# Attention on one core: 16 of 32 head pairs have their Q and K transposed by DMA inside SBUF, and VectorE computes up to eight groups of exponentials

## The chip, the cores and the metric

The kernel runs on one core of a Trainium2 chip. A core has five engines, each with its own stream of instructions: TensorE (PE in the profile; PEld is its weight load), VectorE (DVE), ScalarE (ACT), GpSimd (POOL) and SyncE (SP). SP computes nothing here; it issues the DMA transfers, which 16 DMA engines carry out. [...] each of them, SP included, works through its own program in order. The metric is the device time of one execution in microseconds (us).

## The reference

Plain attention, 8 batches of 8 heads, 512 positions of dimension 64, in and out in float32:

```python
batch, heads, seq, dim = 8, 8, 512, 64
scale = 1.0 / np.sqrt(q.shape[-1])
scores = np.einsum('bhqd,bhkd->bhqk', q, k) * scale
scores = scores - scores.max(axis=-1, keepdims=True)
attn = np.exp(scores)
attn = attn / attn.sum(axis=-1, keepdims=True)
return np.einsum('bhqk,bhkd->bhqd', attn, v)
```

The 64 heads are worked on as 32 pairs (g = 0 to 31). A pair has 8 blocks of scores of 128 keys x 512 queries, and two blocks make a group of 128 x 1024. The kernel skips the maximum: the scores of these inputs are small enough for exp in float32. The row sum comes from a column of ones beside V.

## The kernel before

Each pair goes through these stages: SP loads q, k, v in float32; POOL casts them to fp16 (`qkp`, `vp`); PE transposes q and k, 8 blocks of 128 x 128 into one PSUM bank (`tp`), and DVE copies them to SBUF (`tqk`); PE multiplies the scores (`st`, three PSUM buffers of two banks); ACT takes the exponential into fp16 (`pt`); PE multiplies with V (`o`), seven units of 128 rows to a bank; DVE divides by the row sums into `ring`, and SP stores it.

```python
def feed(g):                      # once a pair, at the first scores of pair g
    load(g + 5, "kqv")
    cast_qk(g + 3)
    cast_v(g + 2)

def transposes(g, n, bank):
    if n == 0:
        tqk[g] = tpool.tile([P, 2, S], FP16, tag="tqk", name=f"tqk_{g}")
        tps[g] = ps_x.tile([P, 2, NI, P], FP16, tag=f"x{bank}", name=f"tp_{g}")
    n = 1 - n
    for i in range(NI):
        nc.tensor.transpose(tps[g][:, n, i, :], qkp[g][:, n, i, :], ident)      # L348

def copy(g):
    ...
    nc.vector.tensor_copy(                                                      # L355
        out=tqk[g][:, :, :], in_=tps.pop(g).rearrange("p n i c -> p n (i c)"))

def scores(m, on_dve):
    ...
        nc.tensor.matmul(st[:, x, :], kc, qc, start=True, stop=True)            # L374
        ...
    if on_dve:
        raised[m] = {"st": st, "pt": pt}
        return
    nc.scalar.activation(                                                       # L379
        out=pt[:, 0:size, :], in_=st[:, 0:size, :], func=EXP, scale=scale)
```

Some groups don't go to ACT: DVE computes their exponential itself. One instruction (`raise_`, L393) reads the scores from PSUM and turns them into an integer whose upper bits are the exponent; six passes (`pass_`: L406 and L417 for the bits, four times L428 for a polynomial of fourth degree) work on it in SBUF. That is seven instructions to a group, and they stand between the copies and the normalisations (L440, L441) of the same engine.

The order of PE's and DVE's instructions is made when the kernel is built. `Plan` steps through a model of the two engines and of ACT, with durations in ns, and writes down what each engine does next; the kernel then issues its instructions in that order.

```python
class Plan:
    SLOT, EXP, EXP_DONE, EXP_FIXED = 216, 853, 1085, 51
    ...
    COPY, NORM, NORM_COLUMN = 700, 380, 67
    RAISE, PASSES, LATE = 1216, (867, 822, 1400, 1400, 1400, 1372), 700
    HURRY = 1200

    def for_dve(self, m):             # does group m go to DVE?
        g = self.groups[m][0][0]
        return (m > 5 and g < self.pairs - 3 and not self.passes
                and not any(x[1] == "raise" for x in self.ready))

    def step_dve(self, t):
        now = [x for x in self.ready if x[0] <= t]
        if now:
            ...                       # a copy, a normalisation or a raise
        elif self.passes:             # else the next pass, if no such work comes soon
            m, s = self.passes[0]
            if min((x[0] for x in self.ready), default=1e9) > t + self.PASSES[s] - self.LATE:
                ...
```

Buffers: six float32 tiles each for q, k and v (`load`), three `qkp`, four `tqk`, thirty `pt` for ACT and three (`pd`) for DVE's groups.

Of the kernel before, what the change touches and what calls it, by code (L numbers as in the profile page):

```python
# [9 lines left out]
FP16 = mybir.dt.float16  # L10
U32 = mybir.dt.uint32

EXP = mybir.ActivationFunctionType.Exp
# [3 lines left out]
class Plan:  # L17
# [10 lines left out]

    SLOT, EXP, EXP_DONE, EXP_FIXED = 216, 853, 1085, 51
    INTO, OUT_OF = 95, 105
    TRANSPOSE, V_UNIT = 225, 130
    TO_ACT, TO_DVE, TO_PE = 275, 210, 60
    COPY, NORM, NORM_COLUMN = 700, 380, 67
    RAISE, PASSES, LATE = 1216, (867, 822, 1400, 1400, 1400, 1372), 700
    HURRY = 1200
    STEP = 5
    FIRST_UNIT = 4

    def __init__(self, groups, pairs, first):
        self.groups, self.pairs = groups, pairs
        self.pe, self.act, self.dve = 6000, 4800 + first * 904, 5800
        self.m, self.tiled = first, True
        self.read = []
        self.exps = {}
        for m in range(first):
            self.exps[m] = 4800 + m * 904 + self.EXP_DONE
            self.read.append(self.exps[m])
        self.tq = {0: 5800}  # L50
        self.next_t = 1
        self.part_t = 0
        self.banks = [5100, 5800]
        self.todo = [(g, h) for g in range(pairs) for h in range(2)]
        self.head = None
        self.units = self.FIRST_UNIT
        self.member = {b: m for m, grp in enumerate(groups) for b in grp}
        self.ready = []
        self.passes = []
        self.steps = []  # L60

    def note(self, t, *what):
# [15 lines left out]
    def for_dve(self, m):  # L78
        g = self.groups[m][0][0]
        return (  # L80
            m > 5
            and g < self.pairs - 3
            and not self.passes
            and not any(x[1] == "raise" for x in self.ready)
        )

    def scores(self, t):
        m, grp = self.m, self.groups[self.m]
        slots = 2 if len(grp) == 2 and 0 < grp[0][0] and grp[0][2] == grp[1][2] else 1
        on_dve = self.for_dve(m)  # L90
        if m % 4 == 0 and grp[0][0] > 0 and len(grp) == 2:
            self.note(t, "feed", grp[0][0])
        self.note(t, "scores", m, on_dve)
        t += (0 if self.tiled else self.INTO) + self.SLOT * slots
        self.tiled = True
        if on_dve:
            self.ready.append((t + self.TO_DVE, "raise", (m,)))
            self.read.append(1e9)
        else:
            begin = max(self.act, t + self.TO_ACT)  # L100
            self.act = begin + self.EXP * len(grp) // 2 + self.EXP_FIXED
            self.exps[m] = self.act + self.EXP_DONE - self.EXP - self.EXP_FIXED
            self.read.append(self.exps[m])
        self.m += 1
        self.pe = t
# [61 lines left out]
    def step_pe(self, t):  # L167
        if self.m == len(self.groups):
            self.values(t)
            return  # L170
        g = self.groups[self.m][0][0]
        backlog = self.act - t
        one, two = self.free() <= t, self.free(1) <= t
        if one and (two or backlog < self.HURRY):
            return self.scores(t)
        if not one and backlog < 1300 and self.free() < t + 150:
            return
        if self.part_t:
            return self.transposes(t)
        if (  # L180
            self.next_t < self.pairs
            and self.next_t <= g + 1
            and t >= self.ready_kq(self.next_t)
            and self.bank(t) is not None
        ):
            return self.transposes(t)
        if not self.values(t) and one:
            self.scores(t)
# [4 lines that stand above are left out]
            job = min(now, key=lambda x: (x[1] != "raise", x[0]))  # L193
            self.ready.remove(job)
            _, kind, what = job
            self.note(t, kind, *what)
            if kind == "norm":
                self.dve = t + self.NORM + self.NORM_COLUMN * what[1]
                self.banks[what[2]] = self.dve + self.TO_PE
            elif kind == "copy":  # L200
                self.dve = t + self.COPY
                self.banks[what[1]] = self.tq[what[0]] = self.dve + self.TO_PE
            else:
                self.dve = t + self.RAISE
                self.read[what[0]] = self.dve + self.TO_PE
                self.passes += [(what[0], s) for s in range(len(self.PASSES))]
        elif self.passes:
            m, s = self.passes[0]
            if min((x[0] for x in self.ready), default=1e9) > t + self.PASSES[s] - self.LATE:
                self.passes.pop(0)  # L210
                self.note(t, "pass", m, s)
                self.dve = t + self.PASSES[s]
                if s == len(self.PASSES) - 1:
                    self.exps[m] = self.dve + self.TO_PE

    def run(self):
        t = 0
# [12 lines left out]
def kernel(  # L230
# [7 lines left out]
    nc = tc.nc  # L238
    B, H, S, D = q.shape
    P = 128  # L240
# [21 lines left out]
    cpool = ctx.enter_context(tc.tile_pool(name="const", bufs=1))  # L262
    lpool = ctx.enter_context(tc.tile_pool(name="load", bufs=6))
    qpool = ctx.enter_context(tc.tile_pool(name="qk16", bufs=3))
    tpool = ctx.enter_context(tc.tile_pool(name="tqk", bufs=4))
    ppool = ctx.enter_context(tc.tile_pool(name="pt", bufs=30))
    dpool = ctx.enter_context(tc.tile_pool(name="pd", bufs=3))
    wpool = ctx.enter_context(tc.tile_pool(name="work", bufs=1))
# [14 lines left out]
    qkp = {}  # L283
    tqk = {}
# [5 lines left out]
    first = {}  # L290
    last = {}

    def source(src, g):
        b, h = g // ppb, 2 * (g % ppb)
        return src[b, h : h + 2].rearrange("h (p i) d -> p h i d", i=NI)

    def load_tile(g, name):
        t = lpool.tile(
            [P, 2, NI, D],
            FP32,  # L300
            tag=f"{name}32",
            name=f"{name}32_{g}",
            bufs=6,
        )
        raw.setdefault(g, {})[name] = t
        return t

    def load(g, names):
        if g >= NP:
            return  # L310
        for name in names:
            src = {"q": q, "k": k, "v": v}[name]
            t = load_tile(g, name)
            if name == "v" and g in HALVED:
                for h in range(2):
                    nc.sync.dma_start(out=t[:, h], in_=source(src, g)[:, h])
                continue
            nc.sync.dma_start(out=t[:, :, :, :], in_=source(src, g))

    def cast_v(g):  # L320
        if g >= NP:
            return
        nc.gpsimd.tensor_copy(out=vps[g % NV][:, :, :, 0:D], in_=raw[g]["v"][:, :, :, :])  # L323

    def cast_qk(g):
        if g >= NP:
            return
        t = qpool.tile([P, 2, NI, P], FP16, tag="qkp", name=f"qkp_{g}")
        for n, name in ((1, "k"), (0, "q")):
            eng = nc.vector if (g, name) == (1, "q") else nc.gpsimd  # L330
            eng.tensor_copy(  # L331
                out=t[:, n].rearrange("p i (h d) -> p h i d", h=2),
                in_=raw[g][name][:, :, :, :],
            )
        qkp[g] = t

    def feed(g):
        load(g + 5, "kqv")
        cast_qk(g + 3)
        cast_v(g + 2)  # L340
# [260 lines left out]
    with tc.manual_schedule():  # L601
        first_loads()
        load(1, "kq")
        load(0, "v")
        for g in range(2, 5):
            load(g, "kq")
            load(g - 1, "v")
        load(4, "v")
        make_identity(nc, ident)
        for n in range(NV):  # L610
            nc.vector.memset(vps[n][:, :, :, D : D + 1], 1.0)
        first_pair()
        cast_qk(1)
        cast_v(0)
        cast_qk(2)
        cast_v(1)
        feed(0)
        do = {
            "transposes": transposes,
            "scores": scores,  # L620
            "values": values,
            "feed": feed,
            "raise": raise_,
            "copy": lambda g, b: copy(g),
            "pass": pass_,
            "norm": lambda u, n, b: normalise(u, n),
        }
        for what, *args in Plan(groups, NP, 3).run():
            do[what](*args)
# [30 lines left out]
```

The softmax here doesn't subtract the row's maximum and nothing guards it: scores larger than these inputs give would overflow.

## Time and profile before

| | |
|---|---|
| device time, median of 3 runs | 123.18 us (123.15 to 123.48) |
| span of the profiled execution | 121.7 us |
| ACT busy | 114.4 us (94%) |
| PE busy, PEld busy | 108.1 us, 67.6 us |
| DVE busy | 98.5 us (81%) |
| POOL busy | 73.9 us (61%) |
| moved by DMA | 33.82 MB, mean 278 GB/s |
| exponentials in ACT's main loop, on DVE | 120 instructions, 6 groups |

A row of groups in the profile reads: line, engine, operation, tile written <- tiles read, partitions x elements, x count | busy us, mean ns of one | idle us of that engine just before them, and what ended most of it. PE's matmuls and ACT's activations overlap their neighbours, so that the mean of one is longer than the step from one to the next. A line of digits divides the span into 40 equal slices and gives the busy share of each in tenths. Releasers, which name what ended a wait, are inferred from semaphores.

### The profile page before, as it was taken

What the parts mean: (1) busy time and instruction counts of PE and PEld (TensorE: products, weight loads), DVE (VectorE), ACT (ScalarE), POOL (GpSimd) and SP (SyncE); (2) the same over time, 40 slices, a digit from 0 to 9 for tenths busy, and PEclk for the clock granted to TensorE, in tenths of its full rate; (3) what the DMA queues carried; (4) which work ended last, traced back from release to release, by engine and by line L of the source; (5) the groups of instructions that cost most, each with busy time, mean ns of one, the idle gap of its engine ahead of it and who ended that gap; (6) DMA issues with size and microseconds to landing.
All of it is one profiled execution on the core that took longest, in us unless ns stands there. A gap on an engine that the chain in (4) does not pass through costs nothing.

```text
span 121.7 us, 3951 instructions
## 1 busy us (share of the span) xinstructions
PE 108.1 (89%) x1557; PEld 67.6 (56%) x1557; DVE 98.5 (81%) x171; ACT 114.4 (94%) x127; POOL 73.9 (61%) x101
## 2 busy tenths in 40 slices
PE   7979788889899798998998998889999998999970
PEld 2556455547466465664565564556655655556550
DVE  1456899989989898699999998986979899876451
ACT  4599999999999999999999999999999999999970
POOL 2368969998487977396587577366794377300000
PEclk9999999999999999999999999999999999999995
DMA  3899999999999989998899967899979995113234
GB/s 117 273 363 384 385 376 384 387 275 282 370 374 352 311 284 318 335 347 276 238 312 297 318 226 251 268 348 343 325 239 281 348 330 196 64 52 126 93 110 152
DMA packets 35603, 33.82 MB, mean 278 GB/s; under 512 B 2688, under 2 KB 35584, under 8 KB 35584
## 3 DMA queue, kind: packets, MB, share of 16 engines
q1 hardware_dynamic: 35152, 33.24, 83.1%
q10 hardware_dynamic: 432, 0.33, 0.9%
q8 instruction: 12, 0.20, 0.7%
q14 instruction: 7, 0.06, 0.2%
HBM read 25.17 MB, written 8.39 MB: 276 GB/s over the span
## 4 chain that ended last, share of the span: by engine, by line
ACT 54%; PE 22%; issue 19%; DVE 2%; ACTq 0%
ACT pt L379 54%; PE st L374 8%; PE o L462 6%; PE st_0a L510 3%; PE tp L348 2%; PE st L553 1%; DVE tqk L353 1%; PE o_last L477 1%; DVE ring L441 1%; PE tp_qb L548 0%; DVE qt L590 0%; DVE obl L490 0%; PE tp_qa L548 0%; PE st_0a L553 0%; DVE rc L440 0%
## 5 line engine op out<-in xcount | busy, mean ns | idle before, releaser
L379 ACT ACTIVATE pt<-st 128x1024 f16<-128x1024 f32 (+1 forms) x120 | 109.4, 1327 | 0.1
L374 PE MATMUL st<-tqk 64*128 64x512 f16 x248 | 48.1, 384 | 7.4 <-ACT pt L379 6.5
L462 PE MATMUL o<-vp,pt 128*128 128x65 f16 x1008 | 46.9, 195 | 1.7 <-ACT pt L379 1.3
L462 PEld LDWEIGHTS <-pt 128*128 128x128 f16 x1008 | 37.0, 98 | 18.8 <-issue 15.0
L331 POOL CAST qkp<-k 128x512 f16<-128x512 f32 x31 | 25.3, 815 | 24.2 <-DMA k<-in_k_dram 18.1
L323 POOL CAST vp<-v 128x512 f16<-128x512 f32 x32 | 27.4, 859 | 1.0 <-DMA v<-in_v_dram 0.9
L374 PEld LDWEIGHTS <-tqk 64*128 64x128 f16 x248 | 13.3, 93 | 20.7 <-issue 12.7
L331 POOL CAST qkp<-q 128x512 f16<-128x512 f32 x30 | 22.7, 756 | 2.4 <-DMA q<-in_q_dram 2.3
L441 DVE TENSOR_TENSOR ring<-o,rc 128x448 f32<-128x448 f32 (+2 forms) x37 | 22.6, 611 | 1.3
L355 DVE COPY tqk<-tp 128x1024 f16<-128x1024 f16 x30 | 20.5, 685 | 3.1 <-PE tp L348 2.8
L348 PE MATMUL tp<-ident,qkp 128*128 128x128 f16 x248 | 19.5, 220 | 0.0
L348 PEld LDWEIGHTS <-qkp 128*128 128x128 f16 x248 | 14.0, 98 | 6.9 <-issue 4.7
L428 DVE SCALAR_TENSOR_TENSOR y<-y,m 128x1024 f32<-128x1024 f32 x12 | 15.9, 1321 | 0.0
L440 DVE RECIPROCAL rc<-o 128x7 f32<-128x7 f32 (+2 forms) x37 | 7.3, 198 | 9.3 <-PE o L462 9.1
L393 DVE TENSOR_SCALAR z<-st 128x1024 uint32<-128x1024 f32 x6 | 7.3, 1221 | 1.1 <-PE st L374 1.1
L428 DVE SCALAR_TENSOR_TENSOR y<-m 128x1024 f32<-128x1024 f32 x6 | 8.2, 1361 | 0.0
L428 DVE SCALAR_TENSOR_TENSOR pt<-y,e 128x1024 f16<-128x1024 f32 x6 | 7.7, 1279 | 0.0
L417 DVE TENSOR_SCALAR e<-z 128x1024 uint32<-128x1024 uint32 x6 | 6.1, 1024 | 0.0
L406 DVE TENSOR_SCALAR m<-z 128x1024 uint32<-128x1024 uint32 x6 | 4.6, 765 | 0.0
L510 PE MATMUL st_0a<-const-bfloat16-1.0 128*128 128x512 bf16 (+1 forms) x11 | 3.5, 482 | 0.8 <-PEq L644 0.8
L510 PEld LDWEIGHTS <-const-bfloat16-1.0 128*128 128x128 bf16 x15 | 1.9, 143 | 2.4 <-issue 2.4
L526 ACT ACT_TABLE_LOAD x1 | 1.3, 1283 | 1.7 <-PEq L644 1.7
(43 smaller groups left out, 18.6 us busy)
## 6 DMA issues: line engine op xcount, KB each, us to landing
out_dram<-ring SPq DMA_DIRECT2D x63, 128.0 KB, 3.8
k<-in_k_dram SPq DMA_DIRECT2D x31, 256.0 KB, 4.8
q<-in_q_dram SPq DMA_DIRECT2D x31, 256.0 KB, 4.9
v<-in_v_dram SPq DMA_DIRECT2D x27, 256.0 KB, 5.3
v<-in_v_dram SPq DMA_DIRECT2D x10, 128.0 KB, 4.4
k<-in_k_dram ACTq DMA_DIRECT2D x2, 128.0 KB, 2.9
q<-in_q_dram SPq DMA_DIRECT2D x2, 128.0 KB, 2.6
out_dram<-obl SPq DMA_DIRECT2D x1, 64.0 KB, 1.8
```

Source lines behind the costliest of these rows:

```text
L323: nc.gpsimd.tensor_copy(out=vps[g % NV][:, :, :, 0:D], in_=raw[g]["v"][:, :, :, :])
L331: eng.tensor_copy(out=t[:, n].rearrange("p i (h d) -> p h i d", h=2), in_=raw[g][name][:, :, :, :],)
L348: nc.tensor.transpose(tps[g][:, n, i, :], qkp[g][:, n, i, :], ident)
L355: nc.vector.tensor_copy(out=tqk[g][:, :, :], in_=tps.pop(g).rearrange("p n i c -> p n (i c)"))
L374: nc.tensor.matmul(st[:, x, :], kc, qc, start=True, stop=True)
L379: nc.scalar.activation(out=pt[:, 0:size, :], in_=st[:, 0:size, :], func=EXP, scale=scale)
L393: nc.vector.tensor_scalar(out=r["z"][:, :, :], in0=r["st"][:, :, :], scalar1=scale * 1.4426950408889634 * 2.0**23, scalar2=(127 + SHIFT) * ...
L428: nc.vector.scalar_tensor_tensor(out=r["pt"][:, :, :] if n == 3 else r["y"][:, :, :], in0=mant if n == 0 else r["y"][:, :, :], scalar=QUAR ...
L440: nc.vector.reciprocal(out=rc[:, 0:n], in_=o[:, x : x + n, D : D + 1])
L441: nc.vector.tensor_tensor(out=ring[:, u % NU : u % NU + n, :], in0=o[:, x : x + n, 0:D], in1=rc[:, 0:n].broadcast_to([P, n, D]), op=AluOp. ...
L462: nc.tensor.matmul(os[u // 7][:, u % 7, :], blocks[(g, c, h)][:, y * P : (y + 1) * P], vps[g % NV][:, h, c, :], start=(c == 0), stop=(c == ...
L510: nc.tensor.matmul(dst[:, 0:n], ones[:, 0:P], ones[:, 0:n], start=True, stop=True)
```

## The change

Of the pairs 5 to 28, those whose number isn't a multiple of three (16 pairs in all, with pair 5 the first) get their transposed q and k by a DMA transpose from `qkp` to `tqk`, inside SBUF. SP issues it at the feed two pairs ahead, before the loads of that feed. PE's transposes and DVE's copy of these pairs fall away, and `tqk` gets a fifth buffer. On DVE, at most eight groups of exponentials are placed (there was no number before; the old order came to six). And the model from which the order is made has new durations: most have two numbers now, one for when the engine can go on and one for when the result is there. The transfers are for taking work from PE and DVE; the room on DVE is for taking exponentials from ACT.

The diff, with cuts marked:

```diff
-    SLOT, EXP, EXP_DONE, EXP_FIXED = 216, 853, 1085, 51
+    SLOT, EXP, EXP_DONE, EXP_FIXED = 216, 853, 181, 64
     ...
-    COPY, NORM, NORM_COLUMN = 700, 380, 67
-    RAISE, PASSES, LATE = 1216, (867, 822, 1400, 1400, 1400, 1372), 700
-    HURRY = 1200
+    COPY, NORM, RAISE = (615, 700), (307, 390), (1145, 1225)
+    NORM_COLUMN, PASS_DONE = 67, 80
+    PASSES = (690, 950, 1335, 1335, 1335, 1250)
+    FIRST_EXP = 5260
     ...
+    BY_DMA = (5, 7, 8, 10, 11, 13, 14, 16, 17, 19, 20, 22, 23, 25, 26, 28)
+    LATE_NORM, LATE_COPY, HURRY, SOON, BACKLOG = 200, 500, 1400, 220, 1000
+    LAST_PAIRS, AHEAD, MARGIN, SLACK, MOST = 3, 0, 1, 2000, 8
     ...
-        self.tq = {0: 5800}
+        self.tq = {0: 5800, **{g: 0 for g in self.BY_DMA}}
     ...  (for_dve)
-            and g < self.pairs - 3
-            and not self.passes
+            and g < self.pairs - self.LAST_PAIRS
+            and len(self.passes) <= self.AHEAD
+            and len(self.on_dve) < self.MOST
     ...  (step_pe)
+        while self.part_t == 0 and self.next_t in self.BY_DMA:
+            self.next_t += 1
     ...
-        if not one and backlog < 1300 and self.free() < t + 150:
+        if not one and backlog < self.BACKLOG and self.free() < t + self.SOON:
     ...  (step_dve)
-            if min((x[0] for x in self.ready), default=1e9) > t + self.PASSES[s] - self.LATE:
+            end = t + int(self.MARGIN * self.PASSES[s])
+            late = {"copy": self.LATE_COPY, "norm": self.LATE_NORM, "raise": self.LATE_NORM}
+            if all(x[0] > end - late[x[1]] for x in self.ready):
     ...
-                    self.exps[m] = self.dve + self.TO_PE
+                    self.exps[m] = end + self.PASS_DONE + self.TO_PE + self.SLACK
     ...
-    tpool = ctx.enter_context(tc.tile_pool(name="tqk", bufs=4))
+    tpool = ctx.enter_context(tc.tile_pool(name="tqk", bufs=5))
     ...
+    def transpose_by_dma(g):
+        if g not in Plan.BY_DMA:
+            return
+        tqk[g] = tpool.tile([P, 2, S], FP16, tag="tqk", name=f"tqk_{g}")
+        nc.sync.dma_start_transpose(
+            out=tqk[g].rearrange("p n (i c) -> p (n i) c", c=P),
+            in_=qkp[g].rearrange("p n i c -> p (n i c)"),
+        )
+
     def feed(g):
+        transpose_by_dma(g + 2)
         load(g + 5, "kqv")
         cast_qk(g + 3)
         cast_v(g + 2)
```

More of the change, by code (lines that the diff above doesn't have):

```diff
@@ L34 @@
     TO_ACT, TO_DVE, TO_PE = 275, 210, 60
-    COPY, NORM, NORM_COLUMN = 700, 380, 67
-    RAISE, PASSES, LATE = 1216, (867, 822, 1400, 1400, 1400, 1372), 700
-    HURRY = 1200
+    COPY, NORM, RAISE = (615, 700), (307, 390), (1145, 1225)
+    NORM_COLUMN, PASS_DONE = 67, 80
+    PASSES = (690, 950, 1335, 1335, 1335, 1250)
+    FIRST_EXP = 5260
     STEP = 5
     FIRST_UNIT = 4
+    BY_DMA = (5, 7, 8, 10, 11, 13, 14, 16, 17, 19, 20, 22, 23, 25, 26, 28)
+    LATE_NORM, LATE_COPY, HURRY, SOON, BACKLOG = 200, 500, 1400, 220, 1000
+    LAST_PAIRS, AHEAD, MARGIN, SLACK, MOST = 3, 0, 1, 2000, 8
     def __init__(self, groups, pairs, first):
         self.groups, self.pairs = groups, pairs
-        self.pe, self.act, self.dve = 6000, 4800 + first * 904, 5800
+        self.pe, self.act, self.dve = 7000, self.FIRST_EXP, 7000
         self.m, self.tiled = first, True
@@ L47, in __init__ @@
         for m in range(first):
-            self.exps[m] = 4800 + m * 904 + self.EXP_DONE
+            self.act += self.EXP + self.EXP_FIXED
+            self.exps[m] = self.act + self.EXP_DONE
             self.read.append(self.exps[m])
-        self.tq = {0: 5800}
+        self.tq = {0: 5800, **{g: 0 for g in self.BY_DMA}}
         self.next_t = 1
@@ L59, in __init__ @@
         self.passes = []
+        self.on_dve = []
         self.steps = []
@@ L96, in scores @@
         if on_dve:
+            self.on_dve.append(m)
             self.ready.append((t + self.TO_DVE, "raise", (m,)))
@@ L101, in scores @@
             self.act = begin + self.EXP * len(grp) // 2 + self.EXP_FIXED
-            self.exps[m] = self.act + self.EXP_DONE - self.EXP - self.EXP_FIXED
+            self.exps[m] = self.act + self.EXP_DONE
             self.read.append(self.exps[m])
@@ L197, in step_dve @@
             if kind == "norm":
-                self.dve = t + self.NORM + self.NORM_COLUMN * what[1]
-                self.banks[what[2]] = self.dve + self.TO_PE
+                more = self.NORM_COLUMN * what[1]
+                self.dve = t + self.NORM[0] + more
+                self.banks[what[2]] = t + self.NORM[1] + more + self.TO_PE
             elif kind == "copy":
-                self.dve = t + self.COPY
-                self.banks[what[1]] = self.tq[what[0]] = self.dve + self.TO_PE
-            else:
-                self.dve = t + self.RAISE
-                self.read[what[0]] = self.dve + self.TO_PE
+                self.dve = t + self.COPY[0]
+                self.banks[what[1]] = self.tq[what[0]] = t + self.COPY[1] + self.TO_PE
+            else:
+                self.dve = t + self.RAISE[0]
+                self.read[what[0]] = t + self.RAISE[1] + self.TO_PE
                 self.passes += [(what[0], s) for s in range(len(self.PASSES))]
@@ L208, in step_dve @@
             m, s = self.passes[0]
-            if min((x[0] for x in self.ready), default=1e9) > t + self.PASSES[s] - self.LATE:
+            end = t + int(self.MARGIN * self.PASSES[s])
+            late = {"copy": self.LATE_COPY, "norm": self.LATE_NORM, "raise": self.LATE_NORM}
+            if all(x[0] > end - late[x[1]] for x in self.ready):
                 self.passes.pop(0)
                 self.note(t, "pass", m, s)
-                self.dve = t + self.PASSES[s]
+                self.dve = end
                 if s == len(self.PASSES) - 1:
-                    self.exps[m] = self.dve + self.TO_PE
+                    self.exps[m] = end + self.PASS_DONE + self.TO_PE + self.SLACK
     def run(self):
```

## The prediction

> **What bounds the kernel now.** I read the page first: busy shares, then the chain that ended last, then the groups; after that the timeline of ScalarE (ACT), the waits of the SyncE queue (SP) and a table by window. The lines that carry it, from the page:
>
> ```profile
> PE 108.1 (89%) x1557; PEld 67.6 (56%) x1557; DVE 98.5 (81%) x171; ACT 114.4 (94%) x127; POOL 73.9 (61%) x101
> DMA  3899999999999989998899967899979995113234
> ...
> ACT 54%; PE 22%; issue 19%; DVE 2%; ACTq 0%
> ...
> L379 ACT ACTIVATE pt<-st 128x1024 f16<-128x1024 f32 (+1 forms) x120 | 109.4, 1327 | 0.1
> ...
> L355 DVE COPY tqk<-tp 128x1024 f16<-128x1024 f16 x30 | 20.5, 685 | 3.1 <-PE tp L348 2.8
> L348 PE MATMUL tp<-ident,qkp 128*128 128x128 f16 x248 | 19.5, 220 | 0.0
> ```
>
> ACT's main group has 109.4 us of busy time and 0.1 us of idle time before its instructions. Its timeline, from the answer on that engine, shows the group as one unbroken piece (start, length), and the whole end of the kernel behind it:
>
> ```profile
> 8.41 109.42 ACT L379 ACTIVATE pt<-st 128x1024 f16<-128x1024 f32 x120
> 119.08 0.37 ACTq L497 DMA_DIRECT2D out_dram<-obl  x1
> ```
>
> So from 8.41 to 117.83 us the exponential is the bound, without a hole. The mean of 1327 ns is not what one costs, because neighbours overlap. 118 of the 120 are full and 2 are half tiles, worth 119 full ones, and 109.42 / 119 = 0.92 us is the step. Everything before 8.41 and the 3.9 us after 117.83 are head and tail, which the change leaves alone.
>
> The windows of the stretch in which pairs are loaded and cast, and of the tail (length, busy of PE, PEld, DVE, ACT, POOL, clock, DMA share, GB/s), show the second resource that is near its limit:
>
> ```profile
> 10.00:98.00 88.00, 80.53 (x1193) 50.81 (x1190) 79.44 (x120) 88.00 (x97) 64.70 (x83) 1.00 0.97 318
> 98.00:121.70 23.70, 19.08 (x307) 12.24 (x304) 15.54 (x29) 19.83 (x23) 4.98 (x7) 0.95 0.42 136
> ```
>
> ACT is busy 88.00 of 88.00 us, and the DMA engines 0.97 at 318 GB/s. They can move more than that: the early slices of the page show 384 to 387 GB/s. The third tight place is SP, which issues every load and store in program order. Its waits in the same stretch, the longest lines:
>
> ```profile
> SPq L449 <- DVE ring L441: 5.9, 8, 1.4
> SPq L318 <- POOL qkp L331: 3.4, 6, 1.1
> SPq L318 <- DMA v<-in_v_dram: 2.9, 9, 0.6
> SPq L449 <- DMA q<-in_q_dram: 2.0, 6, 0.5
> SPq L318 <- DMA q<-in_q_dram: 2.0, 5, 0.8
> ```
>
> With the smaller ones of that answer (1.2, 1.2, 0.7, four times 0.4, 0.2) that makes 21.1 us of waiting in 88 us. The rest is issuing, 0.37 to 0.5 us for each plain transfer in SP's timeline.
>
> [...]
>
> **The change part by part.**
>
> Removed from PE: 16 pairs of 8 transposes. 19.5 / 31 = 0.63 us a pair, 16 x 0.63 = 10.1 us of PE. Worth nothing by itself: PE already feeds ACT with 0.1 us of idle time.
>
> Removed from DVE: 16 copies of PSUM to SBUF, 16 x 0.685 = 11.0 us.
>
> Added to DVE: two more groups of exponentials, 8 in place of 6. From the rows by form, one costs raise 1.221 + mask 0.765 + exponent 1.024 + three multiply passes 1.361 + 2 x 1.321 + last 1.279 = 8.29 us; two are 16.6. Net for DVE: 98.5 + 16.6 - 11.0 = 104.1 us, of a span near 120, or 87%. It fits: DVE now idles 121.7 - 98.5 = 23.2 us.
>
> Removed from ACT: those two groups, 2 x 0.92 = 1.84 us. This is the only part that lies on the path that sets the end. 123.18 - 1.84 = 121.34 us, 1.5% less, and that is a floor: to win 2% (below 120.72) ACT would have to lose a third group or the tail 0.6 us, and the cap on groups is 8.
>
> Added to DMA: 16 x 262 KB = 4.2 MB. Of the 33.82 MB of before, 27.97 lie between 10 and 98 us (the DMA answer for that window). (27.97 + 4.19) MB in 88 - 1.8 us is 373 GB/s, against 384 to 387 at best seen. By rate it just fits, if a transposed byte costs the same as a plain one. [...]
>
> [...]
>
> Reserve: the k casts of pair 31 start at 101.1 us and its PE transposes near 109.0, so raw data lead their use there by 8 us. A transpose by DMA is issued at the feed of two pairs before: a pair takes about (101.1 - 61.1) / (31 - 20) = 3.6 us (k casts of pairs 20 and 31), so it leads its scores by about 7 us, and the median landing of a 256 KB load is 4.8 us. That leaves some 2 us against late landings, less when SP lags.
>
> Moved: the order of PE and DVE comes from new durations. The old model has 904 ns a group for ACT (853 + 51), the new 917 (853 + 64), nearer to the measured 0.92; transposes in DMA are taken as always ready (time 0). DVE passes now may delay a copy by 500 and a normalisation by 200 ns, where both had 700. That guards against an ACT hole, of which there is only 0.1 us to win. The values of a DVE group are planned 2 us later than its last pass, so PE is less likely to stand before it.
>
> **Rivals.**
>
> (a) ACT stays without holes: 121.3 to 121.8 us. For it: PE and the PSUM banks get easier, DVE fits, and the data of a pair are cast in time for the earlier issue (pair 22's k cast starts at 68.67 us, the feed of pair 20 issues at 75.55). The choice of two pairs in three, and none before the fifth, while the first loads run, fits the DMA room above well. My main case, some 60%.
>
> (b) The transposes land late, as DMA engines or SP are full. PE, which runs in order, stands before the scores of such a pair, and ACT gets holes of a fraction of a us in some of 16 places: 122 to 125.6 us. [...] Some 17%.
>
> (c) DMA or SP becomes the bound over the middle of the kernel[...]. The lag passes the 2 us of reserve and then adds in full: 126 to 135 us. For it: nothing else hides behind SP, loads stand in line behind a transpose that waits for its cast. Against it: the reserve of raw data. Some 23%.
>
> (d) DVE becomes the bound and its late groups stall the values: against it 87% and the 2 us of slack. Small.
>
> **Time, range, chances.** The floor is 121.3, the main case with some holes 121.6, and (b) and (c) pull the median up: 121.9 us. The range is 121.1 to 127.5. Faster by over 2% needs more than ACT can give: 0.05. Slower by over 2% is above 125.64: 0.25, which is (c) and the upper end of (b). Within 2%: 0.70.
>
> **What would show it.** Right: 118 activations on the main line in place of 120 with idle still near 0.1 us, ACT's unbroken stretch near 107.6 us, 8 rows of raise, 14 copies of 128 x 1024, DVE near 104 us, SP's waits nearly gone, DMA share near 1 through the middle. Wrong: scores of a pair waiting for a DMA into tqk, ACT waiting for the scores (st), [...] landings far above 5 us, or casts that wait longer for k and q than the 18.1 and 2.3 us of now. If ACT has no holes and the time still isn't 1.84 us less, the step of 0.92 us or the tail has changed, and my sum is wrong there.

## The result, and the profile after

| | before | after |
|---|---|---|
| device time, median | 123.3 us (123.15 to 123.48) | 136.19 us (135.48 to 138.6) |
| ratio | | 1.103 (95% interval 1.098 to 1.107) |
| span of the profiled execution | 121.7 us | 134.4 us |
| exponentials in ACT's main loop, groups on DVE | 120, 6 | 118, 8 |

Ratios, here and below, leave out executions over 1.5% slower than the fastest of the same kernel, medians contain them, so differences between two runs are taken from the ratios.

The page of the kernel after: busy times, DMA by slice, shares of the chain, and the groups that the prediction spoke of.

```profile
PE 106.4 (79%) x1429; PEld 62.8 (47%) x1429; DVE 104.5 (78%) x169; ACT 114.9 (85%) x125; POOL 77.8 (58%) x101
DMA  4999999999999999999999999999999999922234
...
DMA 26%; PE 26%; SPq 12%; POOL 11%; ACT 10%; DVE 8%; issue 4%; POOLq 0%; ACTq 0%
...
L404 ACT ACTIVATE pt<-st 128x1024 f16<-128x1024 f32 (+1 forms) x118 | 109.8, 1046 | 12.2 <-PE st L399 12.0
L399 PE MATMUL st<-tqk 64*128 64x512 f16 x248 | 49.8, 408 | 21.2 <-DMA tqk<-qkp 17.0
...
L380 DVE COPY tqk<-tp 128x1024 f16<-128x1024 f16 x14 | 9.6, 684 | 2.6 <-PE tp L373 2.5
...
tqk<-qkp SPq DMA_TRANSPOSE x16, 4.6
```

The last line says that a transpose landed 4.6 us after its issue in the median.

ACT's share of the chain fell from 54% to 10%. Its idle time went from 0.1 to 12.2 us, nearly all of it waiting for scores; PE waited 17.0 us before those scores for a transposing DMA. The stretch of ACT's main loop, start to end, went from 109.4 to 122.0 us (8.22 to 130.22 in its timeline): two steps of 0.92 us fewer, 12.2 us of holes more, and about 2 us because an activation that has no neighbour takes 1.02 us instead of a step of 0.92.

One such hole, in the timeline around 65 us (start, length, engine, instruction, idle time before it):

```profile
60.05 2.01 SPq L356 DMA_TRANSPOSE tqk<-qkp  x1
...
63.25 0.56 PE L487 MATMUL o<-vp,pt 128*128 128x65 f16 x12
...
65.71 0.39 PE L399 MATMUL st<-tqk 64*128 64x512 f16 x2 [1.89 <-DMA tqk<-qkp]
...
66.14 2.85 ACT L404 ACTIVATE pt<-st 128x1024 f16<-128x1024 f32 x3 [1.43 <-PE st L399]
```

The transpose of pair 16 was issued at 60.05 us and landed 5.6 us later; PE had run out of other work at 63.81. It was issued late because SP was behind: from 43.70 to 60.05 us the rows of SP's timeline follow each other with at most 0.11 us between them. In the same window as before, 10 to 98 us:

```profile
10.00:98.00 88.00, 69.76 (x929) 40.15 (x926) 74.77 (x103) 78.88 (x85) 59.99 (x73) 0.92 1.10 317
```

The DMA engines moved 317 GB/s, as before (318), though transposes were added: what they carry came out of the loads. The share of the DMA engines, the number before it, rose from 0.97 to 1.10; as this profile counts it, it can be above 1. The loads of k of pair 7 and of pair 31 in SP's timeline, two lines before and two after:

```profile
14.04 0.37 SPq L318 DMA_DIRECT2D k<-in_k_dram  x1
...
95.94 0.47 SPq L318 DMA_DIRECT2D k<-in_k_dram  x1
```

```profile
13.63 0.37 SPq L333 DMA_DIRECT2D k<-in_k_dram  x1
...
110.81 0.57 SPq L333 DMA_DIRECT2D k<-in_k_dram  x1
```

That is 81.9 us before (3.41 us a pair) and 97.2 us after (4.05 us a pair). The stream of transfers had become slower than ACT.

### The profile page after: what moved, and what is told of

It reads as the page before. It is cut to its first block, busy times and chain, and to the rows that moved or that the text cites. A ratio compares the mean times of both kernels' runs of the same rounds, so it can differ in the third digit from the quotient of the medians.

```text
span 134.4 us, 3695 instructions
## 1 busy us (share of the span) xinstructions
PE 106.4 (79%) x1429; PEld 62.8 (47%) x1429; DVE 104.5 (78%) x169; ACT 114.9 (85%) x125; POOL 77.8 (58%) x101
## 4 chain that ended last, share of the span: by engine, by line
DMA 26%; PE 26%; SPq 12%; POOL 11%; ACT 10%; DVE 8%; issue 4%; POOLq 0%; ACTq 0%
DMA tqk<-qkp 15%; DMA k<-in_k_dram 11%; ACT pt L404 10%; PE st L399 10%; PE o L487 9%; POOL qkp L346 6%; POOL vp L338 4%; SPq L356 4%; SPq L474 4%; SPq L333 3%; PE tp L373 3%; PE st_0a L535 2%; DVE ring L466 2%; DVE y L453 2%; SPq L331 1%
## 5 line engine op out<-in xcount | busy, mean ns | idle before, releaser
L404 ACT ACTIVATE pt<-st 128x1024 f16<-128x1024 f32 (+1 forms) x118 | 109.8, 1046 | 12.2 <-PE st L399 12.0
L487 PE MATMUL o<-vp,pt 128*128 128x65 f16 x1008 | 52.7, 200 | 1.8 <-ACT pt L404 1.5
L487 PEld LDWEIGHTS <-pt 128*128 128x128 f16 x1008 | 40.1, 101 | 27.2 <-issue 24.2
L346 POOL CAST qkp<-k 128x512 f16<-128x512 f32 x31 | 24.3, 783 | 34.8 <-DMA k<-in_k_dram 31.2
L338 POOL CAST vp<-v 128x512 f16<-128x512 f32 x32 | 31.4, 984 | 1.2 <-DMA v<-in_v_dram 1.1
L453 DVE SCALAR_TENSOR_TENSOR y<-y,m 128x1024 f32<-128x1024 f32 x16 | 21.3, 1329 | 0.1
L380 DVE COPY tqk<-tp 128x1024 f16<-128x1024 f16 x14 | 9.6, 684 | 2.6 <-PE tp L373 2.5
L418 DVE TENSOR_SCALAR z<-st 128x1024 uint32<-128x1024 f32 x8 | 9.7, 1217 | 2.0 <-PE st L399 2.0
L453 DVE SCALAR_TENSOR_TENSOR pt<-y,e 128x1024 f16<-128x1024 f32 x8 | 11.2, 1401 | 0.1
L453 DVE SCALAR_TENSOR_TENSOR y<-m 128x1024 f32<-128x1024 f32 x8 | 10.7, 1334 | 0.0
L373 PE MATMUL tp<-ident,qkp 128*128 128x128 f16 x120 | 10.3, 232 | 0.1
L373 PEld LDWEIGHTS <-qkp 128*128 128x128 f16 x120 | 7.4, 103 | 4.4 <-issue 2.5
```

The source lines that it names most:

```text
L346: eng.tensor_copy(out=t[:, n].rearrange("p i (h d) -> p h i d", h=2), in_=raw[g][name][:, :, :, :],)
L380: nc.vector.tensor_copy(out=tqk[g][:, :, :], in_=tps.pop(g).rearrange("p n i c -> p n (i c)"))
L404: nc.scalar.activation(out=pt[:, 0:size, :], in_=st[:, 0:size, :], func=EXP, scale=scale)
L418: nc.vector.tensor_scalar(out=r["z"][:, :, :], in0=r["st"][:, :, :], scalar1=scale * 1.4426950408889634 * 2.0**23, scalar2=(127 + SHIFT) * ...
L453: nc.vector.scalar_tensor_tensor(out=r["pt"][:, :, :] if n == 3 else r["y"][:, :, :], in0=mant if n == 0 else r["y"][:, :, :], scalar=QUAR ...
L487: nc.tensor.matmul(os[u // 7][:, u % 7, :], blocks[(g, c, h)][:, y * P : (y + 1) * P], vps[g % NV][:, h, c, :], start=(c == 0), stop=(c == ...
```

## The experiments

Three reasons were possible. **A**: the DMA engines are full, a transpose takes more of them than its bytes. **B**: the latency of a transpose, two pairs ahead, closes a loop through SP's order. **C**: SP's queue is full, by the time it takes to issue a transpose. A fourth, **D**, came later: buffers. Times are medians, the ratio is to the kernel before, with its 95% interval.

### Order alone, dead transposes, plain copies, an earlier issue

```diff
# e3: no DMA transposes
-    BY_DMA = (5, 7, 8, ..., 26, 28)
+    BY_DMA = ()
# e4: e3, and the 16 transposes into tiles that nobody reads
+    DEAD = (5, 7, 8, ..., 26, 28)
-        tqk[g] = tpool.tile(...)
+        dead = tpool.tile(...)          # and dma_start_transpose(out=dead..., in_=qkp[g]...)
# e2: a plain copy in place of each transpose (scores of untransposed data)
-        nc.sync.dma_start_transpose(out=tqk[g]..., in_=qkp[g]...)
+        nc.sync.dma_start(out=tqk[g][:, :, :], in_=qkp[g]...)
# e1: three pairs ahead, six tqk buffers
-        transpose_by_dma(g + 2)        # first in feed
+        transpose_by_dma(g + 3)        # behind cast_qk(g + 3)
```

> The new model and order with no DMA transpose at all; the plan then places seven groups on VectorE. Both theories: the order isn't what costs, one exponential less on ACT gives 123.3 - 0.92 = 122.4 us (122 to 123). A third theory, that the new order itself starves ACT: above 125 us.

> As the run with the order alone, and beside it the same 16 transposing DMAs at the same places of SP's queue, into tiles that nobody reads; PE's own transposes stay. Theory A: the engines carry the same bytes and packets, so loads come late all the same: 130 us or more. Theory B: nobody waits for a landing, so 122.4 to 125 us.

> The transposing DMA is replaced by a plain DMA copy of the same 262 KB from qkp to tqk, at the same place and with the same waits (scores of those pairs are then those of untransposed data). Theory A: a plain copy takes about 0.7 us of the engines where the transpose takes 1.8, which gives back some 17 us of the loading stretch: below 124 us. Theory B: only the issue gets shorter (about 0.5 us instead of 1.4), so the loop goes from 8.2 to about 7.2 us for two pairs; 125 to 129 us remain.

> Each transposing DMA is issued one pair earlier, three pairs ahead and behind the cast of the same feed, with six tqk buffers. Theory A (the DMA engines are full: a transpose takes about 1.8 us of all of them, worked out as 102 us of loading stretch less 27.97 MB at 384 GB/s, divided by 16): an earlier issue frees no capacity, so the time stays at 133 us or more. Theory B (a loop through SP's order: scores, values, normalisation, store, transpose two pairs ahead, scores, 8.2 us around for two pairs where ACT needs 6.8): a third pair of lead opens the loop, PE's wait for tqk (17 us) nearly goes, and the time is 121.5 to 125 us.

Measured: e3 123.86 us (1.006, 1.003 to 1.008), e4 135.6 (1.093, 1.088 to 1.097), e2 129.22 (1.049, 1.043 to 1.055), e1 136.01 (1.105, 1.099 to 1.111).

The order isn't what costs: with seven groups and no DMA transpose it is 0.6% above the kernel before. Used transposes cost 12.0 us over e3, dead ones 10.7, so the wait for their landing makes little of the loss. An earlier issue gave nothing: PE's wait for transposes only fell from 17.0 to 14.2 us, and the time stayed. So B falls as the main cause. The plain copy, expected below 124 us by A, took 129.2 and cost 5.4 us over e3. A by itself isn't of that size; B's 125 to 129 nearly was, but B is out by e4.

### SP's time without bytes, fewer bytes, a transpose by itself

```diff
# e5: three tiny DMAs in place of each dead transpose
+        for n in range(3):
+            nc.sync.dma_start(out=tiny[0:16, x + n, :], in_=ident[0:16, 0:16])
# e6: e4 with stores of 16 of 128 partitions (the rest of the output is left out)
-    out=source(out, g)[:, h], in_=ring[:, ...]
+    out=source(out, g)[0:16, h], in_=ring[0:16, ...]
# e7: no attention; 16 transposes, then 16 plain copies of the same size, from SP
```

> As the run with dead transposes, but each transpose is replaced by three tiny plain DMAs (16 partitions x 32 bytes, inside SBUF), which keep SP's queue for about 3 x 0.45 = 1.35 us as a transpose does, move nearly nothing and wait for no cast. Theory A (the DMA engines' time): as the order alone, 123 to 125 us. Theory C (SP's queue is what is full, by the 1.4 us that each transpose takes to issue): as the dead transposes, 131 us or more.

> The dead transposes stay, and every store from the ring moves only 16 of its 128 partitions (the rest of the output is left out): SP issues as many transfers as before, but 5 to 7 MB less cross the DMA engines, some 14 to 19 us of them at 384 GB/s. Theory A: most of the loss goes, 123 to 127 us. Theory C: no change, 133 us or more.

> Attention is left out entirely: 16 transposing DMAs of 262 KB one after the other from SP with nothing else in flight, then 16 plain copies of the same size inside SBUF. Theory A: the transposes need about 1.7 us of the engines each even alone (some 28 us, 150 GB/s), the copies 0.7 us (370 GB/s). Theory C: the transposes come at the rate at which SP issues them, 1.4 us, with the DMA engines idle in between.

Measured: e5 141.2 us (1.136, 1.130 to 1.142), e6 131.45 (1.066, 1.061 to 1.070). The windows of e5, as above:

```profile
10.00:98.00 88.00, 75.73 (x1037) 45.54 (x1036) 73.12 (x110) 79.38 (x86) 52.47 (x68) 0.96 0.80 253
```

48 transfers of half a KB each cost more than 16 transposes, with the DMA engines at 0.80 and 253 GB/s: SP's time alone is enough to starve the kernel. (Each took SP 0.59 us, not the 0.45 assumed.) But with 7.2 MB fewer bytes (30.79 in place of 38.02 MB in all) and as many issues, e6 gave back 3.3 us of the 10.7 that dead transposes cost: bytes count too. e7 by SP's timeline, and its windows, first three in the transposes, the last in the copies (DVE and POOL busy, clock, DMA share, GB/s):

```profile
1.95 21.58 SPq L631 DMA_TRANSPOSE dst<-src  x16
25.52 10.28 SPq L638 DMA_DIRECT2D dst<-gate  x16
```

```profile
3.00:10.00 7.00, 0.00 (x0) 0.00 (x0) 1.00 0.83 188
10.00:20.00 10.00, 0.00 (x0) 0.00 (x0) 1.00 0.88 198
...
28.00:36.00 8.00, 0.00 (x0) 0.00 (x0) 1.00 1.04 402
```

16 transposes take SP 21.58 us, 1.35 each, without a gap, while the engines aren't full: alone they are bound by their issue. At a share of 0.83 to 0.88 they hold the engines an estimated 0.85 x 1.35 = 1.15 us each, where a plain copy at 402 GB/s needs 0.65 us.

### Freeing SP, freeing buffers, fewer transposes

```diff
# e9, e10, e11: a load from pair 6 on brings two pairs in one DMA (after, e3, e1)
-        load(g + 5, "kqv")
+        (load if g == 0 else load_two)(g + 5, "kqv")
# e13: e11 with 6 qkp and 7 tqk buffers; e14: e13 with stores of 16 partitions
# e16: e1 with these buffers, loads of one pair
# e15: eight transposes (its plan leaves one of the 64 heads unstored)
-    BY_DMA = (5, 7, 8, 10, ...)
+    BY_DMA = (5, 8, 11, 14, 17, 20, 23, 26)
```

> The changed kernel with its 16 transposes, but from pair 6 on each load brings two pairs in one DMA (39 loads of 512 KB in place of 78 or more of 256 and 128 KB; tiles hold two pairs, room for eight pairs in place of six). The same bytes cross the DMA engines. Theory C (SP's queue is full): 39 to 44 issues fewer, at 0.5 us some 20 us of SP, nearly what 16 transposes add (16 x 1.45 = 23 us); the time falls to 121.5 to 126 us. Theory A (the engines' time): 132 us or more.

> Control: the same merging of loads without any DMA transpose (order alone, seven groups on VectorE). Theory C: SP was not full there, so as the order alone, 123.3 to 124.3 us. If merging loads is worth something by itself, it shows here: below 123.

> Merged loads, and the transposes issued three pairs ahead in place of two. Theory C alone: as the merged loads, since the queue is what counts. With the latency of a transpose as a second limit (Theory B): 1 us or more below the merged loads, down to the floor of 121.3 us.

> Merged loads, transposes three pairs ahead, six qkp buffers in place of three and seven tqk: SP's queue and the buffers are both relieved, the bytes stay. Theory D (loops through buffers and latency were what remained): 121.5 to 124 us. Theory A (engines: 16 x 1.15 us as measured alone and 73 us of plain traffic at 384 GB/s are 91 us, in a stretch of 86): at least 5 us over the floor, 126 us or more.

> As the run before, and every store from the ring moves only 16 of 128 partitions (the rest of the output is left out): 5 to 7 MB less in the stretch. Theory A: the last limit is gone, 121.5 to 124 us, whatever the run before gave. Theory D: as the run before within 1 us.

> Single loads, transposes three pairs ahead, six qkp and seven tqk buffers. Theory C (SP's queue): it is as full as before, so 132 us or more. Theory D: the buffers were the limit, 121.5 to 126 us.

> The changed kernel with eight transposes (every third pair from 5 to 26), single loads, lead and buffers as in the change; the plan places seven groups on VectorE. If a fixed room counts (SP 21 us of waiting against 8 x 1.45 = 12; engines 73 + 8 x 1.15 = 82 us of 86): 123 to 125 us, as the order alone. If each transpose costs by its own latency: half of the loss over the order alone, 129 to 131 us.

| run | us | ratio (95%) |
|---|---|---|
| e9, merged loads | 137.95 | 1.110 (1.103 to 1.118) |
| e10, the same, no transposes | 124.25 | 1.006 (1.004 to 1.009) |
| e11, merged, three pairs ahead | 140.6 | 1.138 (1.130 to 1.146) |
| e13, merged, ahead, buffers | 141.64 | 1.147 (1.140 to 1.154) |
| e14, e13 with small stores | 133.22 | 1.077 (1.068 to 1.085) |
| e16, ahead, buffers | 137.03 | 1.101 (1.094 to 1.109) |
| e15, eight transposes | 130.88 | 1.062 (1.056 to 1.069) |

C alone falls with e9: SP issued 44 transfers fewer and nothing was won. D falls with e13 and e16: buffers and lead made nothing better. With small stores, e14 gained 8.7 us over e13, half of what A expected, and stayed 8.7 us above e10. And eight transposes cost 7.0 us over e3 against 12.0 for sixteen, where a fixed room would have let eight through for nothing; what these 7 us were is read further down.

### SP's stream by itself

```diff
# e17: no attention, no waits on engines; five stretches of 12 pairs: two stores of 128 KB,
#      then nothing | a transpose | three tiny DMAs, then loads of k, q, v (merged in the last two)
```

> Attention is left out: SP alone issues, without waiting for any engine, five stretches of 12 pairs each, per pair three loads of 256 KB and two stores of 128 KB. Plain: 2.7 to 2.9 us a pair (1.05 MB at 360 to 385 GB/s). With one transpose a pair: Theory A, 1.15 us more as alone or 1.8 as worked out, 3.9 to 4.6 us; Theory C, 5 x 0.5 + 1.4 = 3.9 us. With three tiny transfers instead: Theory A, 2.7 to 3.1 us with SP keeping up; Theory C, 5 x 0.5 + 3 x 0.59 = 4.3 us. With loads merged for two pairs and one transpose a pair: Theory A, as unmerged, 3.9 to 4.6 us; Theory C, about (3 x 0.55 + 4 x 0.45 + 2 x 1.4) / 2 = 3.1 us. For ACT, a pair lasts 3.4 us.

One pair of the second stretch and two pairs of the fifth, in SP's timeline:

```profile
78.49 0.47 SPq L662 DMA_DIRECT2D v<-in_v_dram  x1
79.00 0.94 SPq L635 DMA_DIRECT2D out_dram<-ring  x2
79.99 1.49 SPq L640 DMA_TRANSPOSE t<-src  x1
81.52 0.66 SPq L662 DMA_DIRECT2D k<-in_k_dram  x1
82.22 0.50 SPq L662 DMA_DIRECT2D q<-in_q_dram  x1
...
241.97 2.84 SPq L640 DMA_TRANSPOSE t<-src  x1
244.85 1.05 SPq L635 DMA_DIRECT2D out_dram<-ring  x2
245.95 1.72 SPq L640 DMA_TRANSPOSE t<-src  x1
247.71 0.58 SPq L656 DMA_DIRECT2D k<-in_k_dram  x1
```

And the five stretches in windows (share of the engines and GB/s are the last two numbers):

```profile
8.16:38.54 30.38, 0.00 (x0) 0.00 (x0) 1.00 1.03 338
53.53:95.47 41.94, 0.00 (x0) 0.00 (x0) 1.00 1.10 309
112.38:157.31 44.93, 0.00 (x0) 0.00 (x0) 1.00 0.80 234
177.79:200.00 22.21, 0.00 (x0) 0.00 (x0) 1.00 1.09 371
220.00:255.00 35.00, 0.00 (x0) 0.00 (x0) 1.00 1.09 306
```

From start to start of the same transfer in the timeline, a pair takes 2.99 us plain, 4.17 with a transpose, 4.49 with three tiny transfers (each over eleven steps), 2.84 merged, and 4.25 merged with a transpose (8.5 us for two). The ten steps of the first three windows, without the start on an empty queue, give 3.04, 4.19 and 4.49. In the second stretch SP has no gap over 0.06 us left, but for one of 0.42: five plain issues at about 0.51 us and 1.45 us of transpose are 4.0. The plain ones take no longer there (0.94 us for two stores, then 0.58, 0.48 and 0.47 for k, q and v in the median) than in the third stretch (0.94, 0.58, 0.47, 0.47), where the engines are at 0.80, so SP is the limit. In the fifth, SP has fewer issues, and the pair is no shorter: now the issue of every second transpose stretches to 2.8 us, with the engines at 1.09. So A and C are both true, at almost the same rate: freeing SP alone leads from 4.17 us to the engines' 4.25, and in the third stretch SP is the limit as in e5.

The kernel shows it too. The issues of its 16 transposes (shortest, median and longest, ns), in the kernel after and then in e9:

```profile
L356 SPq DMA_TRANSPOSE tqk<-qkp x16: 1237/1384/2105, 17.2 to 108.7; - x16
```

```profile
L372 SPq DMA_TRANSPOSE tqk<-qkp x16: 1327/2324/3600, 17.6 to 110.0; - x16
```

In SP's timeline they add up to 24.1 us after and 35.9 in e9: over half of the estimated 22 us (44 issues of 0.5) that merging had freed went into them, and in e13 their median was 2.99 us.

With two pairs in three, the stream by itself takes 2.99 / 3 + 4.17 x 2 / 3 = 3.78 us a pair, against 3.41 us that a pair lasted in the kernel before. In the kernel, the loads of k came at these rates (first and last time in SP's timeline, as above):

| | stream by itself, us a pair | loads in the kernel | more |
|---|---|---|---|
| after, 16 transposes | 3.78 | 4.05 | 0.27 |
| e15, eight (2.99 x 2 / 3 + 4.17 / 3) | 3.38 | 3.71 | 0.33 |
| e5, tiny (2.99 / 3 + 4.49 x 2 / 3) | 3.99 | 4.43 | 0.44 |

About 0.3 to 0.4 us a pair come on top in all three. A likely reason is that SP stands in its order behind stores and transposes whose data another engine hasn't finished; no run shows it by itself.

For e15 the mean over 24 pairs misleads. Its timeline, ACT's lines first:

```profile
29.52 58.12 ACT L404 ACTIVATE pt<-st 128x1024 f16<-128x1024 f32 x63 [0.44 <-PE st L399]
91.86 1.02 ACT L404 ACTIVATE pt<-st 128x1024 f16<-128x1024 f32 x1 [4.22 <-PE st L399]
```

```profile
84.40 1.92 SPq L356 DMA_TRANSPOSE tqk<-qkp  x1
...
91.15 0.61 PE L399 MATMUL st<-tqk 64*128 64x512 f16 x2 [4.39 <-DMA tqk<-qkp]
```

From 29.52 to 87.64 us, with five transposes issued and landed, ACT ran without a hole at its step of 0.92 us. Of the 7.5 us of holes in all, 4.22 are one: a transpose went out behind three stores at 84.40 and landed 6.7 us later, while PE stood before its scores. So at one transpose in three pairs the stream kept up for most of the time, and the larger part of the loss was a late landing, as in B. The steady lag is shown for sixteen transposes only.

### Two orders without transposes in the stream

```diff
# e8: e3 with two other numbers in the plan; e12: e8 with merged loads
-    ..., HURRY, SOON, BACKLOG = ..., 1400, 220, 1000
+    ..., HURRY, SOON, BACKLOG = ..., 1400, 220, 1300
-    LAST_PAIRS, AHEAD, MARGIN, SLACK, MOST = 3, 0, 1, 2000, 8
+    LAST_PAIRS, AHEAD, MARGIN, SLACK, MOST = 3, 0, 1, 0, 8
# e18: e8 with transposes where the loads are over
-    BY_DMA = ()
+    BY_DMA = (29, 30, 31)
```

> No DMA transposes; the order alone with two numbers of the plan changed: no slack behind a VectorE group's last pass (2000 to 0 ns) and a backlog limit of 1300 in place of 1000 ns. The order alone won 0.86 us on ACT (main stretch ended at 116.97 in place of 117.83 us) and lost 1 us in the tail, where 56 matmuls of values stood behind the last exponential; with the slack gone the values of the last VectorE group come earlier. Expected 122.4 to 123.0 us, just faster than before. If the tail isn't what took the gain: 123.5 to 124 as the order alone.

> Merged loads with the seven-group plan that has no slack behind the last pass and no DMA transposes (122.63 us with single loads). Theory C: within 0.4 us of that, 122.2 to 123.

> The seven-group plan without slack (122.63 us), but pairs 29 to 31 are transposed by DMA: their transfers fall at about 99 to 107 us, when the loads are over. If only the room on SP and the DMA engines counts, they cost nothing: 122.3 to 123.0 us. If a transpose brings a stall wherever it stands (0.75 us each, as 12.3 us by 16): about 124.9 us.

Measured: e8 122.63 us (0.994, 0.991 to 0.996), e12 123.12 (0.998, 0.996 to 0.999), e18 123.13 (1.000, 0.998 to 1.001). ACT's main loop in e3 and then in e8:

```profile
9.55 107.42 ACT L404 ACTIVATE pt<-st 128x1024 f16<-128x1024 f32 x118 [0.49 <-PE st L399]
119.25 0.35 ACTq L522 DMA_DIRECT2D out_dram<-obl  x1
```

```profile
9.56 107.42 ACT L404 ACTIVATE pt<-st 128x1024 f16<-128x1024 f32 x118 [0.75 <-PE st L399]
118.46 0.37 ACTq L522 DMA_DIRECT2D out_dram<-obl  x1
```

Both end ACT's work near 116.97 us, 0.86 before the kernel before (117.83): one exponential fewer is worth about what a step is. e3 gave it back behind ACT, where the last store was issued 2.3 us later; in e8 it is 1.5 us. So e8 is 0.6% faster than the kernel before and the fastest version here; e12, with merged loads, is 0.2% faster. In these two traces ACT also has a hole of 0.5 to 0.75 us at its second group. Three transposes where no loads are left (e18, issued at 100.99, 103.05 and 105.48 us, the last load at 97.39) cost 0.7 us over e8, just outside the range expected if they were free, where 2.2 were expected of a fixed price for each. In its profiled execution ACT's work ended at 116.97 us too, so nothing of this is on ACT, and nothing is won by them.

## Why the prediction was wrong

- The step of ACT, "2 x 0.92 = 1.84 us", held as a size: e3 and e8 show one group's worth, 0.86 us. In the kernel after it drowned in 12.2 us of holes.
- DVE: 104.5 us busy against 104.1 predicted, 14 copies, 8 raised groups. Right, and never a limit. Rival (d) stayed out.
- The step that failed is "By rate it just fits", with the belief that SP's waits are room (below) beside it. It set all traffic against 384 to 387 GB/s, the rate of early slices (9.1 to 24.3 us) in which SP issues 17 loads and 4 stores, where a pair later has three loads and two stores. Loads with stores run at 2.99 us a pair (1.05 MB, 350 GB/s) by themselves, and a transpose adds 1.2 to 1.4 us among them (4.17 - 2.99, 4.25 - 2.84), not the 0.7 that its 262 KB make at 373 to 387 GB/s. Over 24 pairs that is 24 x 2.99 + 16 x 1.2 = 91 us of stream in a stretch of 82.
- That SP had room for the transposes was the author's estimate; no trace of before shows what one costs it. Measured it is a median of 1.38 us in the kernel, 1.35 alone, 24.1 us in all. What was wrong was to hold 21.1 us of waiting to be room. In the kernel after, the waits listed for SP in the same window make 13.5 us, 8.3 of them at eight transposes, for casts. In the timeline only one of these eight, 1.5 us before the transpose at 17.19 us, stands ahead of its issue; the other seven overlap it. The 14 transposes issued in the window took 20.7 us, and the listed waits shrank by 7.6.
- "The reserve of raw data" of 8 us was a stock, and a stream that lags 0.64 us a pair (4.05 - 3.41) over 24 pairs, 15 us, uses up any stock.
- Rival (c), "126 to 135 us", named the mechanism and had 23%, though the measured 136.2 lies above its end; the main case had 60% because the choice of two pairs in three looked measured. That was a reading of intentions, not of the profile. (b), late landings, were mostly a symptom with sixteen transposes, as dead ones cost 10.7 of 12.0 us; with eight (e15) one late landing was the larger part of the loss.
- "DMA or SP": it is both. Where the last 0.3 to 0.4 us a pair come from, and why more buffers and lead made merged loads 4.5 us worse (e13 against e9), stays open.

## What to carry to other kernels

A queue that feeds a saturated engine has a price list: measure it by itself, per unit of work, with the real mix of loads, stores and extra transfers, and compare with the pace of the engine, before moving work into it. Idle time of a queue that waits for other engines wasn't room here, and a utilisation that is near 1 with its throughput below the best seen is a warning, not a reserve. Work that costs a free engine 0.6 us can be dear at 1.2 us of a full one.

## What was not expected of the hardware

- A DMA of half a KB kept SP no shorter than a load of 256 KB: 0.59 us (e5; 0.60 in e17's third stretch) against 0.47 to 0.58 us for the loads of that stretch.
- A transpose inside SBUF held the engines an estimated 1.15 us alone (e7, share of 0.85 x 1.35 us; 262 KB, about 230 GB/s), a plain copy of the same bytes 0.65 us (402 GB/s).
- After four of the times that PE stood still in the kernel after (2.35, 1.89, 2.64 and 1.61 us, the last ending at 113.92), its granted clock fell to 0.50 in a window of 2 us, and a pair of score matmuls then took up to 0.61 us instead of 0.39. After two others, of 1.69 and 1.61 us (ending at 29.97 and 40.87), it stayed at 1.00. So the length of the stop alone doesn't decide it, and what does isn't shown here. The lines are windows behind the stop of 1.89 us, then behind that of 1.69 (PE, PEld, DVE, ACT, POOL busy, clock, DMA share, GB/s).

```profile
66.00:68.00 2.00, 1.57 (x19) 0.76 (x18) 0.58 (x1) 1.86 (x3) 1.44 (x3) 0.80 1.10 373
68.00:70.00 2.00, 2.00 (x21) 1.31 (x18) 0.83 (x2) 1.75 (x3) 0.29 (x1) 0.50 1.17 350
```

```profile
30.00:32.00 2.00, 2.00 (x28) 1.01 (x29) 1.97 (x2) 1.60 (x2) 1.32 (x2) 1.00 1.09 382
32.00:34.00 2.00, 0.94 (x14) 0.56 (x12) 1.97 (x5) 2.00 (x3) 1.41 (x2) 1.00 1.18 338
```
